# Four rows of an expert's matrix per partition: 2 MB transfers into nine double slots

## The chip, the cores and the metric

The kernel runs on one core of one Trainium2 chip. A core has five engines that run side by side: TensorE (PE; its weight loads are listed apart as PEld), VectorE (DVE), ScalarE (ACT), GpSimd (POOL) and SyncE (SP), which issues most of the DMA transfers; 16 DMA engines move the data. The metric is the device time of one execution in microseconds, as the median of several runs.

## What is computed

One decoder layer for 256 tokens of width 1024 in f32: sliding-window attention and a gated chunk mixer, a mixture of experts, a second mixer with a recurrent state, and a feed-forward block. The change lies in the mixture of experts. 32 experts have three 1024 x 1024 matrices each (384 MB of f32 in all), and each token goes to four experts:

```python
def routed_experts(x, w_router, b_router, w_gate, b_gate, w_up, b_up, w_down, b_down):
    logits = (xt @ w_router + b_router).astype(jnp.float32)
    top_vals, top_idx = lax.top_k(logits, TOP_K)          # TOP_K = 4
    gates = jax.nn.softmax(top_vals, axis=-1)
    ...
    def expert_block(args):
        xb, e = args
        gt = jnp.minimum(xb @ w_gate[e] + b_gate[e], SWIGLU_LIMIT)
        up = jnp.clip(xb @ w_up[e] + b_up[e], -SWIGLU_LIMIT, SWIGLU_LIMIT)
        hid = gt * jax.nn.sigmoid(SWIGLU_ALPHA * gt) * (up + 1.0)
        return hid @ w_down[e] + b_down[e]
    ...
    out = jnp.zeros((T + 1, D), x.dtype).at[row_tok].add(y_rows * row_gate[:, None])[:T]
```

## The kernel before

The stages follow each other: `front` (attention, gated mixer, router; up to about 125 us), `moe` (the experts; to about 1068 us), `mixer2` (to about 1365 us) and `ffn2` (to the end).

**Weights.** Every expert matrix is read as four *pieces* of 1 MB, 384 pieces in all. `expert_pieces` (L634) lists them in the order of use: gate and up of expert e, then down of expert e-1, and so on. A piece holds 256 rows of the matrix, and its view `(i p x) c -> i p x c` with x = 2 puts rows 256i + 2p and 256i + 2p + 1 into partition p, so that each partition reads one run of 8 KB. The pieces go into 18 slots of 128 x 2048 f32 in a ring (`SLOTS_A`, six, and `SLOTS_B`, twelve). The first 18 pieces are issued while `front` still runs, by `pump` (L1259); all later ones by `fetch`, which calls `piece` (L182; the DMA is L188, on SyncE's queue). `ahead(n)` (L923) calls `fetch` for all pieces up to 18 beyond those already used, once per expert ahead of gate and up (8 pieces) and once ahead of down (4 pieces). So a transfer is issued as soon as the matmuls on the slot's former piece are done. The DMAs of a queue share eight semaphores in turn, so that one is issued only when the eighth before it has landed (the DMAHW waits in the rows of order below).

**Products.** Tokens are chosen per expert by a one-hot matrix. For each pair of experts, `gather` (L710) multiplies h with it, with h as the weights that TensorE loads: 8 chunks of 128 columns by 2 halves of the tokens, 32 matmuls (tiles `tr<-oh,h` and `sc<-oh,h`). Since partition p holds every second row of a piece, chunk k takes every second column of h, by `pairs(k)` (L628). In the same manner `hidden_t` (L768) transposes the hidden values sg of one expert by 4 instructions (L81, `tr<-ident,sg`). `product` then runs 32 matmuls on the four pieces of a matrix (tiles g, u and y, L77), 8 on each.

**The overflow branch.** After expert 15 (`REST`), all engines meet at a loop over tokens that didn't fit (L851), which runs no times here. Before it SyncE waits for every transfer issued so far (206 pieces, of which 192 are used by then). The loop cuts the experts' stage into two segments: pieces 18 to 205 ahead of it, 206 to 383 behind it. Behind the loop the gather of the next pair comes first.

**After the experts.** The constants of the next stage go into two ring slots (`small`), and the front and the later stages use the same slots for their own weights (`raw_slots`, `half_slots`, given out by `pump`).

Of the kernel before, what the change touches and what calls it, by code (L numbers as in the profile page):

```python
# [12 lines left out]
F32 = mybir.dt.float32  # L13
F32R = mybir.dt.float32r
# [16 lines left out]

SLOTS_A = "r8 c1 c0 c2 c3 c4".split()
SLOTS_B = "r0 r1 r2 r3 r4 r5 r6 r7 h0 h1 h2 h3".split()

REST = 15
RING_A = len(SLOTS_A)
FFN_RAW, FFN_HALF = 4, 4
# [18 lines left out]
def bcast_rows(ap, n, parts=128):  # L56
    return bass.AP(tensor=ap.tensor, offset=ap.offset, ap=[[0, parts], [1, n]])


class Net:  # L60
# [120 lines left out]

    def piece(self, src, name="w"):  # L182

        pool, i = self.rings[self.turn % len(self.rings)]
        self.turn += 1
        t = pool.tile([128, 2048], F32, tag=i, name=self.nm(name))
        for view, ap in src(t):
            self.nc.sync.dma_start(view, ap)  # L188
        return t

    def front(self, fctx):
# [18 lines left out]

        slot = {i: (p, f"s{i}") for p, names in ((self.pa, SLOTS_A), (self.pb, SLOTS_B)) for i in names}
        cs = [slot[f"c{i}"][0].tile([128, 2048], F32, tag=f"sc{i}", name=f"front_c{i}") for i in range(5)]

# [39 lines left out]
        nf = len(spec)  # L253
        work = self.expert_pieces()
        spec += [(2, src) for _, src in work[:len(slot)]]
        L = {}
# [74 lines left out]
        def freed():  # L331
            self.freed()
            if len(self.half) == len(halves):
                self.raw_slots += self.half_slots
                self.half_slots = []
                self.pump()

# [267 lines left out]
        assert len(self.raw) == len(spec) and not self.raw_slots  # L605
        self.rings = [self.held[nf + i] for i in range(len(slot))]
        self.turn = len(slot)
        self.work = work
        self.got = {key: t for (key, _), t in zip(work, self.raw[nf:])}

# [16 lines left out]
    @staticmethod  # L627
    def pairs(k):  # L628


        i, x = divmod(k, 2)
        return slice(256 * i + x, 256 * i + 256, 2)

    def expert_pieces(self):  # L634

        r = []
        for e in range(NE + 1):
            for x, names in ((e, ("w_gate", "w_up")), (e - 1, ("w_down",)), (e, ("w_down",))):
                if x in range(NE) and (len(names) == 2 or (x == e) == (x == REST)):
                    for nme in names:  # L640
                        v = self.a[nme][0, x].rearrange("(i p x) c -> i p x c", p=128, x=2)
                        r += [((x, nme, i), v[i]) for i in range(4)]
        return r

    def fetch(self, n):

        for key, src in self.work[len(self.got):n]:
            t = self.piece(lambda t: [(t.rearrange("p (k c) -> p k c", k=2), src)])
            self.got[key] = t.rearrange("p (k c) -> p k c", k=2)

    def moe(self, mctx):
# [52 lines left out]
        def gather(b):  # L704
            xg[b] = m2.tile([128, KC, EB * CAP], F32, tag="xg", bufs=1, name=self.nm("xg"))
            for c0 in range(0, KC, 4):
                p = bank(*(("sc", 2) if c0 else ("tr", 1)), [128, 4, EB * CAP])
                for c in range(4):
                    for t in range(NT):
                        self.mm(p[:, c, :], self.h[:, t, self.pairs(c0 + c)],  # L710
                                oh[b][:, t].rearrange("p e s -> p (e s)"), start=t == 0, stop=t == NT - 1)
                nc.vector.tensor_copy(xg[b][:, c0:c0 + 2, :], p[:, 0:2])
                nc.scalar.copy(xg[b][:, c0 + 2:c0 + 4, :], p[:, 2:4])
# [50 lines left out]
        def hidden_t(sg):  # L764
            hidT = m2.tile([128, 4, 2, CAP], F32, tag="hidT", bufs=1, name=self.nm("hidT"))
            p = bank("tr", 1, [128, 4, 128])
            for j in range(4):
                self.tr(p[:, j, :], sg[:, self.pairs(j)])  # L768
            nc.scalar.copy(hidT[:, 0:2].rearrange("p j f s -> p j (f s)"), p[:, 0:2])  # L769
            nc.vector.tensor_copy(hidT[:, 2:4].rearrange("p j f s -> p j (f s)"), p[:, 2:4])  # L770
            return hidT
# [7 lines left out]
        def weights_of(e, nme):  # L779
            return lambda k: self.got[e, nme, k // 2][:, k % 2, :]  # L780

# [67 lines left out]
        def overflow():  # L849
            n = nc.values_load(lists["num"][0:1, 0:1], min_val=0, max_val=NL - 1)  # L850
            with tc.For_i(0, n, 1) as i:  # L851
# [15 lines left out]
                for k in range(KC):  # L867
                    for t in range(NT):
                        self.mm(p[:, k, :], self.h[:, t, self.pairs(k)], oh[:, t], start=t == 0, stop=t == NT - 1)
                nc.vector.tensor_copy(xo, p)  # L870

                def weights(nme):
                    def f(k):
                        w = m2.tile([128, D], F32, tag="wx", bufs=1, name=self.nm("wx"))
                        rows = a[nme][0, bass.ds(e, 1)].rearrange("o (i p x) c -> i x (o p) c", p=128, x=2)
                        nc.sync.dma_start(w, rows[k // 2, k % 2])
# [98 lines left out]

        def small(*names):
            while self.rings[self.turn % len(self.rings)][0] is self.pa:
                self.turn += 1
            t = self.piece(lambda t: [(t[:, i * D:(i + 1) * D], bcast_rows(a[nme], D)) for i, nme in enumerate(names)])
            return t[:, 0:D], t[:, D:2 * D]  # L980
# [220 lines left out]
    def stream(self):  # L1201
# [23 lines left out]
        for f in range(NF + 2):  # L1225
            for q in range(3):
# [3 lines left out]
                if u % 2 == 0:  # L1230
# [5 lines left out]
                               else (lambda t, x=x: t[:, x:x + 1, :])))  # L1236
        self.pieces(spec, halves, [(self.pa, f"s{i}") for i in SLOTS_A[:2]])
        self.half_slots = [(self.pa, f"s{i}") for i in SLOTS_A[2:]]
        self.low = [self.nc.gpsimd]
# [8 lines left out]
    def pump(self):  # L1248

        nc = self.nc  # L1250
        while True:
            while self.raw_slots and len(self.raw) < len(self.spec):
                r = len(self.raw)
                k, src = self.spec[r]
                pool, tag = self.held[r] = self.raw_slots.pop(0)
                n = src.shape[2]
                t = pool.tile([128, 2048], F32, tag=tag, name=self.nm("w"))[:, :k * n]
                t = t.rearrange("p (k c) -> p k c", k=k)
# [8 lines left out]
            k, n = src.shape[1:]  # L1267
            pool, tag = slot = self.half_slots.pop(0)
            t = pool.tile([128, 2, 1024], F32R, tag=tag, name=self.nm("wp"))[:, :, :k * n]
            t = t.rearrange("p q (k c) -> p q k c", k=k)  # L1270
# [650 lines left out]
    def ffn2(self):  # L1921
# [3 lines left out]
        with ExitStack() as c:  # L1925
# [79 lines left out]
```

## Time and profile before

| | us |
|---|---|
| median of 3 runs | 1569.32 (1568.11 to 1570.33) |
| the profiled execution | 1571.36 |
| its span | 1569.3 |
| TensorE's matmuls busy | 1423.9 (91%) |
| VectorE busy | 600.2 (38%) |
| ScalarE busy | 364.1 (23%) |

The page cuts the span into 40 slices of 39 us. For each it gives what the DMA engines moved in GB/s. The rows further below come from this and from closer views of the trace: stretches with their DMA share, waits, and the timeline of an engine, where equal instructions in a row stand in one line with their count. A time in brackets behind a row is the idle time before it, with what ended it.

### The profile page before, as it was taken

What the parts mean: (1) busy time and instruction counts of PE and PEld (TensorE: products, weight loads), DVE (VectorE), ACT (ScalarE), POOL (GpSimd) and SP (SyncE); (2) the same over time, 40 slices, a digit from 0 to 9 for tenths busy, and PEclk for the clock granted to TensorE, in tenths of its full rate; (3) what the DMA queues carried; (4) which work ended last, traced back from release to release, by engine and by line L of the source; (5) the groups of instructions that cost most, each with busy time, mean ns of one, the idle gap of its engine ahead of it and who ended that gap; (6) DMA issues with size and microseconds to landing.
All of it is one profiled execution on the core that took longest, in us unless ns stands there. A gap on an engine that the chain in (4) does not pass through costs nothing. (4 is left out here: it accounts for less than half of the span.)

```text
span 1569.3 us, 19400 instructions
## 1 busy us (share of the span) xinstructions
PE 1423.9 (91%) x7904; PEld 825.2 (53%) x7904; DVE 600.2 (38%) x1087; ACT 364.1 (23%) x607; POOL 177.6 (11%) x155
## 2 busy tenths in 40 slices
PE   8779999999998865999999989997987999999998
PEld 7664333333333222333333332326876887799998
DVE  4882121122121110121223221215578556876664
ACT  4551010100101000001001010003544233365552
POOL 4630000000000002000000000003443214200000
PEclk9988999999999997999999999998999999999999
DMA  9786999999999998999999999993523124675540
GB/s 303 277 330 259 422 418 422 421 421 421 421 421 422 421 421 311 422 421 421 421 421 421 421 421 421 421 420 119 177 88 117 32 76 172 209 247 178 193 143 27
DMA packets 119279, 491.14 MB, mean 313 GB/s; under 512 B 16391, under 2 KB 46791, under 8 KB 70036
## 3 DMA queue, kind: packets, MB, share of 16 engines
q1 hardware_dynamic: 118304, 489.02, 78.6%
q8 instruction: 63, 1.03, 0.3%
q0 software_dynamic: 512, 0.20, 0.1%
q10 hardware_dynamic: 372, 0.66, 0.1%
q14 instruction: 28, 0.23, 0.0%
HBM read 488.34 MB, written 1.51 MB: 312 GB/s over the span
## 5 line engine op out<-in xcount | busy, mean ns | idle before, releaser
L77 PE MATMUL g<-w,xg 128*64 128x512 f32 x1024 | 239.1, 618 | 4.8 <-DMA w<-in_w_gate_dram 4.8
L77 PE MATMUL u<-w,xg 128*64 128x512 f32 x1024 | 228.6, 594 | 9.9 <-DMA w<-in_w_up_dram 9.9
L77 PE MATMUL y<-w,hidT 128*64 128x512 f32 x1024 | 226.5, 594 | 1.9 <-ACT hidT L769 1.0
L1272 DVE TENSOR_TENSOR wp<-w,wp 128x1024 fp32r<-128x1024 f32 x115 | 153.0, 1355 | 106.7 <-ACT wp L1271 106.6
L1271 ACT CAST wp<-w 128x1024 fp32r<-128x1024 f32 (+1 forms) x148 | 151.6, 1038 | 167.1 <-PE pj L77 63.7
L77 PEld LDWEIGHTS u<-w,xg 128*64 128x64 f32 x1024 | 70.2, 137 | 157.8 <-issue 125.3
L77 PEld LDWEIGHTS g<-w,xg 128*64 128x64 f32 x1024 | 73.8, 143 | 149.5 <-issue 129.1
L77 PEld LDWEIGHTS y<-w,hidT 128*64 128x64 f32 x1024 | 70.9, 137 | 151.1 <-issue 139.9
L1272 POOL TENSOR_TENSOR wp<-w,wp 128x1024 fp32r<-128x1024 f32 (+1 forms) x33 | 78.6, 2386 | 575.0 <-DMA w<-in_w_in_dram 447.7
L777 ACT COPY y<-y 64x512 f32<-64x512 f32 x64 | 37.1, 580 | 369.1 <-PE y L77 368.7
L757 DVE TENSOR_SCALAR g<-g 128x512 f32<-128x512 f32 x32 | 22.1, 691 | 228.1 <-PE g L77 228.1
L770 DVE COPY hidT<-tr 128x256 f32<-128x256 f32 x32 | 13.6, 424 | 230.4 <-ACT hidT L769 230.4
L760 DVE TENSOR_SCALAR g<-u 128x512 f32<-128x512 f32 x32 | 22.1, 691 | 168.2 <-PE u L77 168.1
L77 PE MATMUL pj<-wp,h2p 128*128 128x512 f32 x336 | 82.9, 402 | 2.1 <-DVE wp L1272 1.9
L758 ACT ACTIVATE sg<-g 128x512 f32<-128x512 f32 x32 | 20.2, 630 | 253.3 <-DVE g L757 253.3
L77 PEld LDWEIGHTS pj<-wp,h2p 128*128 128x128 f32 x336 | 62.8, 191 | 18.5 <-DVE wp L1272 2.7
L77 PE MATMUL a<-h3p,wp 128*128 128x256 f32 x528 | 66.9, 283 | 0.5 <-DVE h3p L1307 0.5
L77 PEld LDWEIGHTS a<-h3p,wp 128*128 128x128 f32 x528 | 66.0, 191 | 2.2 <-DVE h3p L1307 0.7
L77 PE MATMUL b<-h3p,wp 128*128 128x256 f32 x528 | 66.9, 283 | 0.0
L77 PEld LDWEIGHTS b<-h3p,wp 128*128 128x128 f32 x528 | 64.9, 192 | 0.0
L77 PE MATMUL tr<-oh,h 128*128 128x128 f32 x256 | 37.7, 306 | 29.9 <-DVE oh L700 29.9
L77 PE MATMUL sc<-y,ogT 128*128 128x512 f32 x124 | 62.5, 619 | 2.5 <-ACT y L777 1.4
(527 smaller groups left out, 1609.0 us busy)
## 6 DMA issues: line engine op xcount, KB each, us to landing
w<-in_w_gate_dram SPq DMA_DIRECT2D x128, 1024.0 KB, 19.8
w<-in_w_up_dram SPq DMA_DIRECT2D x128, 1024.0 KB, 19.8
w<-in_w_down_dram SPq DMA_DIRECT2D x128, 1024.0 KB, 19.8
w<-in_w_in_dram SPq DMA_DIRECT2D x27, 1024.0 KB, 5.1
w<-in_w_ffn_up_dram SPq DMA_DIRECT2D x22, 1024.0 KB, 5.2
w<-in_w_ffn_down_dram SPq DMA_DIRECT2D x11, 1024.0 KB, 7.7
w<-in_w_out_dram SPq DMA_DIRECT2D x8, 1024.0 KB, 8.2
w<-in_w_branch_b_dram SPq DMA_DIRECT2D x2, 1024.0 KB, 4.9
```

The source lines that it names most:

```text
L77: return self.nc.tensor.matmul(out, lhsT, rhs, start=start, stop=stop)
L757: nc.vector.tensor_scalar(g1, pg, 7.0, None, op0=OP.min)
L758: nc.scalar.activation(sg, g1, AF.Sigmoid, scale=1.702)
L760: nc.vector.tensor_scalar(g1, pu, -7.0, 7.0, op0=OP.max, op1=OP.min)
L770: nc.vector.tensor_copy(hidT[:, 2:4].rearrange("p j f s -> p j (f s)"), p[:, 2:4])
L777: nc.scalar.copy(yv[64 * i:64 * i + 64, hf * 512:(hf + 1) * 512], py[64 * hf:64 * hf + 64, :])
L1271: nc.scalar.copy(t[:, 0], src)
L1272: self.low[j % len(self.low)].tensor_tensor(t[:, 1], src, t[:, 0].bitcast(F32), op=OP.subtract)
```

## The change

Each partition gets four neighbouring rows of a matrix: the view has x = 4, a half of a matrix (2 MB) is one transfer, and each partition reads one run of 16 KB. The ring has nine slots of 128 x 4096 in place of eighteen of 128 x 2048. The first 18 pieces and the last four are still transfers of 1 MB: a piece is then half of a partition's four rows (a run of 8 KB out of each 16 KB), and it goes into half of a double. `ahead` counts in doubles, so each call issues the same bytes as before. Since partition p holds rows 4p to 4p + 3 of a half, chunk k now takes every fourth column of h and of sg (`rows_of`), in as many instructions as before. The constants of the next stage go into one double.

```diff
-SLOTS_A = "r8 c1 c0 c2 c3 c4".split()
-SLOTS_B = "r0 r1 r2 r3 r4 r5 r6 r7 h0 h1 h2 h3".split()
+PAIRS = "r2r3 r4r5 r6r7 r8c1 c0c2 c3c4 r0r1 h2h3 h0h1".split()
+PAIRS_A = PAIRS[3:6]
+
+EARLY = 2 * len(PAIRS)
...
-    def piece(self, src, name="w"):
-
-        pool, i = self.rings[self.turn % len(self.rings)]
-        self.turn += 1
-        t = pool.tile([128, 2048], F32, tag=i, name=self.nm(name))
-        for view, ap in src(t):
-            self.nc.sync.dma_start(view, ap)
-        return t
+    def double(self, name, dtype=F32):
+
+        return (self.pa if name in PAIRS_A else self.pb).tile([128, 4096], dtype, tag=name, name=self.nm("w"))
+
+    @staticmethod
+    def halved(t):
+        return [Slot(t[:, 2048 * x:2048 * x + 2048]) for x in range(2)]
...
-    def pairs(k):
-
-
-        i, x = divmod(k, 2)
-        return slice(256 * i + x, 256 * i + 256, 2)
-
-    def expert_pieces(self):
+    def rows_of(k):
+
+
+        i, x = divmod(k, 4)
+        return slice(512 * i + x, 512 * i + 512, 4)
+
+    def expert_quarters(self):
...
-                        v = self.a[nme][0, x].rearrange("(i p x) c -> i p x c", p=128, x=2)
-                        r += [((x, nme, i), v[i]) for i in range(4)]
+                        v = self.a[nme][0, x].rearrange("(i p x) c -> i p x c", p=128, x=4)
+                        r += [((x, nme, q), v[q // 2][:, 2 * (q % 2):2 * (q % 2) + 2, :]) for q in range(4)]
...
     def fetch(self, n):
 
-        for key, src in self.work[len(self.got):n]:
-            t = self.piece(lambda t: [(t.rearrange("p (k c) -> p k c", k=2), src)])
-            self.got[key] = t.rearrange("p (k c) -> p k c", k=2)
+        while self.turn < n and 2 * self.turn < len(self.work):
+            u = 2 * self.turn
+            t = self.double(PAIRS[self.turn % len(PAIRS)]).rearrange("p (k c) -> p k c", k=4)
+            self.turn += 1
+            (key, src), (key1, src1) = self.work[u:u + 2]
+            if u < len(self.work) - 4:
+                e, nme, q = key
+                v = self.a[nme][0, e].rearrange("(i p x) c -> i p x c", p=128, x=4)
+                self.nc.sync.dma_start(t, v[q // 2])
+            else:
+                self.nc.sync.dma_start(t[:, 0:2], src)
+                self.nc.sync.dma_start(t[:, 2:4], src1)
+            self.have(key, t[:, 0:2])
+            self.have(key1, t[:, 2:4])
...
-                        self.mm(p[:, c, :], self.h[:, t, self.pairs(c0 + c)],
+                        self.mm(p[:, c, :], self.h[:, t, self.rows_of(c0 + c)],
...
-                self.tr(p[:, j, :], sg[:, self.pairs(j)])
+                self.tr(p[:, j, :], sg[:, self.rows_of(j)])
...
-            self.fetch(done[0] + len(self.rings))
-            done[0] += n
+            self.fetch(done[0] + len(PAIRS))
+            done[0] += 2 * n
...
-            ahead(4)
+            ahead(1)
...
-            ahead(8)
+            ahead(2)
...
-        self.ln2g, self.ln2b = small("ln2_g", "ln2_b")
-        self.n1g, self.junk = small("norm1_g_2")
+        while PAIRS[self.turn % len(PAIRS)] in PAIRS_A:
+            self.turn += 1
+        t = self.double(PAIRS[self.turn % len(PAIRS)])
+        self.ln2g, self.ln2b, self.n1g, self.junk = (t[:, i * D:(i + 1) * D] for i in range(4))
+        for view, nme in ((self.ln2g, "ln2_g"), (self.ln2b, "ln2_b"), (self.n1g, "norm1_g_2")):
+            nc.sync.dma_start(view, bcast_rows(a[nme], D))
```

On SyncE, where the first pieces of the ring's second round are issued (w_down is expert 0's, then come gate and up of expert 1; a wait for DMAHW is for an earlier transfer on that semaphore, a wait for PE is for the slot), the rows before are:

```order
L1259 DMA w_1066<-in_w_down_dram 128x2048 [waits DMAHW2_49,PE_49]
L1259 DMA w_1074<-in_w_down_dram 128x2048 [waits DMAHW3_49,PE_49]
L188 DMA w_1295<-in_w_down_dram 128x2048 [waits DMAHW4_49,PE_49]
L188 DMA w_1297<-in_w_down_dram 128x2048 [waits DMAHW5_49,PE_49]
L188 DMA w_1299<-in_w_gate_dram 128x2048 [waits DMAHW6_49,PE_49]
L188 DMA w_1301<-in_w_gate_dram 128x2048 [waits DMAHW7_49,PE_49]
```

In the changed kernel the same stretch reads:

```order
L1290 DMA w_1028<-in_w_down_dram 128x2048 [waits DMAHW2_49,PE_49]
L1290 DMA w_1028<-in_w_down_dram 128x2048 [waits DMAHW3_49]
L676 DMA w_1250<-in_w_down_dram 128x4096 [waits DMAHW4_49,PE_49]
L676 DMA w_1252<-in_w_gate_dram 128x4096 [waits DMAHW5_49,PE_49]
L676 DMA w_1254<-in_w_gate_dram 128x4096 [waits DMAHW6_49,PE_49]
```

One row of 128x4096 stands for two of 128x2048, and its wait for PE covers both halves of the slot.

On SyncE just ahead of the overflow branch (`onum` is the number of tokens that didn't fit), the rows before are:

```order
L188 DMA w_3099<-in_w_gate_dram 128x2048 [waits DMAHW4_49,PE_49]
L188 DMA w_3101<-in_w_gate_dram 128x2048 [waits DMAHW5_49,PE_49]
L188 DMA w_3103<-in_w_up_dram 128x2048 [waits DMAHW6_49,PE_49]
L188 DMA w_3105<-in_w_up_dram 128x2048 [waits DMAHW7_49,PE_49]
L850 TENSOR_LOAD onum [waits DVE_49]
L850 ISA x2
```

And in the changed kernel:

```order
L676 DMA w_2828<-in_w_gate_dram 128x4096 [waits DMAHW7_49,PE_49]
L676 DMA w_2870<-in_w_gate_dram 128x4096 [waits DMAHW0_49,PE_49]
L676 DMA w_2872<-in_w_up_dram 128x4096 [waits DMAHW1_49,PE_49]
L882 TENSOR_LOAD onum [waits DVE_49]
L882 ISA x2
```

The same two pieces of w_up are the last ones ahead of the branch, now as one transfer. On the other engines the instructions stand in the same order as before.

## Rows read from the trace of the kernel before

**Rows 1.** The page's 40 slices: GB/s that the DMA engines moved.

```profile
GB/s 303 277 330 259 422 418 422 421 421 421 421 421 422 421 421 311 422 421 421 421 421 421 421 421 421 421 420 119 177 88 117 32 76 172 209 247 178 193 143 27
```

**Rows 2.** Stretches: engines' busy us (instructions), granted clock, DMA share, GB/s.

```profile
200.00:300.00 100.00, 95.76 (x454) 37.15 (x456) 22.24 (x50) 9.71 (x20) 2.26 (x4) 0.98 1.01 420
1098.00:1100.00 2.00, 2.00 (x20) 2.00 (x19) 1.16 (x3) 0.88 (x3) 1.97 (x1) 1.00 1.03 399
1146.00:1148.00 2.00, 2.00 (x10) 1.65 (x9) 2.00 (x3) 0.78 (x1) 0.59 (x1) 1.00 1.02 386
```

**Rows 3.** SyncE's queue: line, waited for: us in total, times, longest us.

```profile
SPq L188 <- DMA w<-in_w_down_dram: 204.7, 100, 2.5
...
SPq L188 <- PE g L77: 97.1, 42, 19.6
```

**Rows 4.** SyncE's timeline at the experts' start, and one stretch there.

```profile
127.14 2.04 SPq L188 DMA_DIRECT2D w<-in_w_down_dram  x2
...
150.66 2.24 SPq L188 DMA_DIRECT2D w<-in_w_up_dram  x2
...
150.00:155.00 5.00, 5.00 (x24) 1.52 (x22) 0.00 (x0) 0.00 (x0) 0.00 (x0) 0.91 0.65 215
```

**Rows 5.** Timeline around the overflow branch, TensorE.

```profile
573.76 3.89 PE L77 MATMUL sc<-y,ogT 128*128 128x512 f32 x8 [0.68 <-ACT y L777]
606.66 3.78 PE L77 MATMUL tr<-oh,h 128*128 128x128 f32 x16 [29.01 <-DVE oh L700]
```

**Rows 6.** TensorE's timeline in segment 2: gathers and the end of u 31.

```profile
753.54 2.15 PE L77 MATMUL tr<-oh,h 128*128 128x128 f32 x16
...
757.41 4.12 PE L77 MATMUL sc<-y,ogT 128*128 128x512 f32 x8
...
809.30 2.15 PE L77 MATMUL tr<-oh,h 128*128 128x128 f32 x16
...
863.36 2.15 PE L77 MATMUL tr<-oh,h 128*128 128x128 f32 x16
...
922.16 2.15 PE L77 MATMUL tr<-oh,h 128*128 128x128 f32 x16
...
981.82 2.15 PE L77 MATMUL tr<-oh,h 128*128 128x128 f32 x16
...
1039.60 1.94 PE L77 MATMUL u<-w,xg 128*64 128x512 f32 x8 [0.56 <-DMA w<-in_w_up_dram]
1041.47 1.98 PE L77 MATMUL sc<-y,ogT 128*128 128x512 f32 x4
```

**Rows 7.** TensorE's waits from 127 to 606 us.

```profile
PE u L77 <- DMA w<-in_w_up_dram: 4.0, 8, 0.6
PE g L77 <- DMA w<-in_w_gate_dram: 2.8, 6, 0.6
...
PE y L77 <- DMA w<-in_w_down_dram: 0.4, 1, 0.4
```

**Rows 8.** Weight loads of transposes (L81): ns min/median/max, first and last start.

```profile
L81 PEld LDWEIGHTS tr<-ident,sg x128: 194/209/226, 145.5 to 1052.9; 128*128 128x128 f32 x128
...
L81 PEld LDWEIGHTS tr<-ident,og x32: 138/142/144, 139.3 to 999.5; 128*128 128x128 f32 x32
```

**Rows 9.** TensorE's timeline in mixer2: contiguous transposes.

```profile
1178.65 0.60 PE L81 MATMUL s<-ident,cs 128*128 128x128 f32 x4
1179.08 0.60 PE L81 MATMUL s<-ident,e 128*128 128x128 f32 x4
```

**Rows 10.** VectorE's groups by form, 1160 to 1190 us: busy us, mean ns.

```profile
L1543 DVE TENSOR_TENSOR z<-s,mask 128x384 f32<-128x384 f32 x8 | 3.9, 544 | 0.3 <-PE s L77 0.3
...
L1565 DVE TENSOR_TENSOR h<-h,rsi 128x512 f32<-128x512 f32 x1 | 0.7, 673 | 0.0
L1550 DVE TENSOR_TENSOR TA<-TA 128x225 f32<-128x225 f32 x1 | 0.6, 565 | 0.0
...
L1550 DVE TENSOR_TENSOR TA<-TA 128x144 f32<-128x144 f32 x1 | 0.4, 405 | 0.0
```

More of the change, by code (lines that the diff above doesn't have):

```diff
@@ L29 @@
 NEG = -1e30
-SLOTS_A = "r8 c1 c0 c2 c3 c4".split()
-SLOTS_B = "r0 r1 r2 r3 r4 r5 r6 r7 h0 h1 h2 h3".split()
+PAIRS = "r2r3 r4r5 r6r7 r8c1 c0c2 c3c4 r0r1 h2h3 h0h1".split()
+PAIRS_A = PAIRS[3:6]
+EARLY = 2 * len(PAIRS)
 REST = 15
-RING_A = len(SLOTS_A)
 FFN_RAW, FFN_HALF = 4, 4
@@ L57, in bcast_rows, with __init__, room @@
     return bass.AP(tensor=ap.tensor, offset=ap.offset, ap=[[0, parts], [1, n]])
+class Slot:
+    def __init__(self, view=None, pool=None, tag=None, dtype=F32):
+        self.view, self.pool, self.tag, self.dtype = view, pool, tag, dtype
+    def room(self, name):
+        return self.view if self.pool is None else self.pool.tile([128, 2048], self.dtype, tag=self.tag, name=name)
 class Net:
@@ L208, in front @@
         self.warm(bank("o", [128, 128]), warm, WARM[2])
-        slot = {i: (p, f"s{i}") for p, names in ((self.pa, SLOTS_A), (self.pb, SLOTS_B)) for i in names}
-        cs = [slot[f"c{i}"][0].tile([128, 2048], F32, tag=f"sc{i}", name=f"front_c{i}") for i in range(5)]
+        slot = {}
+        for name in PAIRS:
+            slot[name[:2]], slot[name[2:]] = self.halved(self.double(name, F32R if name[0] == "h" else F32))
+        cs = [slot[f"c{i}"].view for i in range(5)]
         def carve(i, at, shape):
@@ L253, in front @@
         nf = len(spec)
-        work = self.expert_pieces()
-        spec += [(2, src) for _, src in work[:len(slot)]]
+        work = self.expert_quarters()
+        spec += [(2, src) for _, src in work[:EARLY]]
         L = {}
@@ L332, in freed @@
             self.freed()
[L333 to L336, printed above, removed]
+            for name in PAIRS[-2:]:
+                pair = [slot[name[:2]], slot[name[2:]]]
+                if len(self.half) == len(halves) and all(i in self.half_slots for i in pair):
+                    self.half_slots = [i for i in self.half_slots if i not in pair]
+                    slot[name[:2]], slot[name[2:]] = self.halved(self.double(name))
+                    through(name[:2], name[2:])
         def through(*names):
@@ L605, in front @@
         assert len(self.raw) == len(spec) and not self.raw_slots
[L606 to L609, printed above, removed]
+        order = [slot[h] for t in PAIRS for h in (t[:2], t[2:])]
+        assert [self.held[nf + i] for i in range(EARLY)] == order
+        self.work, self.turn, self.got = work, len(PAIRS), {}
+        for (key, _), t in zip(work, self.raw[nf:]):
+            self.have(key, t)
     def split_biases(self, bf):
@@ L640, in expert_pieces, with have @@
                     for nme in names:
-                        v = self.a[nme][0, x].rearrange("(i p x) c -> i p x c", p=128, x=2)
-                        r += [((x, nme, i), v[i]) for i in range(4)]
-        return r
+                        v = self.a[nme][0, x].rearrange("(i p x) c -> i p x c", p=128, x=4)
+                        r += [((x, nme, q), v[q // 2][:, 2 * (q % 2):2 * (q % 2) + 2, :]) for q in range(4)]
+        return r
+    def have(self, key, t):
+        for x in range(2):
+            self.got[key[:2] + (2 * key[2] + x,)] = t[:, x, :]
     def fetch(self, n):
-        for key, src in self.work[len(self.got):n]:
-            t = self.piece(lambda t: [(t.rearrange("p (k c) -> p k c", k=2), src)])
-            self.got[key] = t.rearrange("p (k c) -> p k c", k=2)
+        while self.turn < n and 2 * self.turn < len(self.work):
[12 more added lines that the diff above has]
+            self.have(key1, t[:, 2:4])
     def moe(self, mctx):
@@ L779, in weights_of @@
         def weights_of(e, nme):
-            return lambda k: self.got[e, nme, k // 2][:, k % 2, :]
+            return lambda k: self.got[e, nme, k]
         def gate_up(e):
@@ L868, in overflow @@
                     for t in range(NT):
-                        self.mm(p[:, k, :], self.h[:, t, self.pairs(k)], oh[:, t], start=t == 0, stop=t == NT - 1)
+                        self.mm(p[:, k, :], self.h[:, t, self.rows_of(k)], oh[:, t], start=t == 0, stop=t == NT - 1)
                 nc.vector.tensor_copy(xo, p)
@@ L874, in f @@
                         w = m2.tile([128, D], F32, tag="wx", bufs=1, name=self.nm("wx"))
-                        rows = a[nme][0, bass.ds(e, 1)].rearrange("o (i p x) c -> i x (o p) c", p=128, x=2)
-                        nc.sync.dma_start(w, rows[k // 2, k % 2])
+                        rows = a[nme][0, bass.ds(e, 1)].rearrange("o (i p x) c -> i x (o p) c", p=128, x=4)
+                        nc.sync.dma_start(w, rows[k // 4, k % 4])
                         return w
@@ L974, in moe @@
         finish(NE - 1)
[L976 to L980, printed above, removed]
-        self.ln2g, self.ln2b = small("ln2_g", "ln2_b")
-        self.n1g, self.junk = small("norm1_g_2")
+        while PAIRS[self.turn % len(PAIRS)] in PAIRS_A:
[4 more added lines that the diff above has]
+            nc.sync.dma_start(view, bcast_rows(a[nme], D))
         flush(sums)
@@ L1236, in stream @@
                                else (lambda t, x=x: t[:, x:x + 1, :])))
-        self.pieces(spec, halves, [(self.pa, f"s{i}") for i in SLOTS_A[:2]])
-        self.half_slots = [(self.pa, f"s{i}") for i in SLOTS_A[2:]]
+        raw, *parts = PAIRS_A
+        self.pieces(spec, halves, self.halved(self.double(raw)))
+        self.half_slots = [h for t in parts for h in self.halved(self.double(t, F32R))]
         self.low = [self.nc.gpsimd]
@@ L1254, in pump @@
                 k, src = self.spec[r]
-                pool, tag = self.held[r] = self.raw_slots.pop(0)
+                slot = self.held[r] = self.raw_slots.pop(0)
                 n = src.shape[2]
-                t = pool.tile([128, 2048], F32, tag=tag, name=self.nm("w"))[:, :k * n]
+                t = slot.room(self.nm("w"))[:, :k * n]
                 t = t.rearrange("p (k c) -> p k c", k=k)
@@ L1267, in pump @@
             k, n = src.shape[1:]
-            pool, tag = slot = self.half_slots.pop(0)
-            t = pool.tile([128, 2, 1024], F32R, tag=tag, name=self.nm("wp"))[:, :, :k * n]
+            slot = self.half_slots.pop(0)
+            t = slot.room(self.nm("wp")).rearrange("p (q n) -> p q n", q=2)[:, :, :k * n]
             t = t.rearrange("p q (k c) -> p q k c", k=k)
@@ L1932, in bank @@
                 return ps.tile(shape, F32, tag=tag, bufs=bufs, name=self.nm(tag))
-            self.raw_slots += [(ph, f"r{i}") for i in range(FFN_RAW)]
+            self.raw_slots += [Slot(pool=ph, tag=f"r{i}") for i in range(FFN_RAW)]
             self.pump()
@@ L1942, in ffn2 @@
             self.low = [V]
-            self.half_slots += [(ph, f"h{i}") for i in range(FFN_HALF)]
+            self.half_slots += [Slot(pool=ph, tag=f"h{i}", dtype=F32R) for i in range(FFN_HALF)]
             self.pump()
```

## The prediction

> **What bounds the kernel now.** I read the slices of the page first, then the speed by stretch, then who waits for whom. From 125 to 1041 us the experts' 384 MB pass through the core, and the slices of GB/s stand at 420 to 422 in all that time but for the one at 155 and the one at 600 [rows 1]; 200 to 300 us give 420 GB/s at a share of 1.01, so all 16 DMA engines are full [rows 2]. SyncE's queue waits there for an earlier transfer to land (204.7 us in 100 waits for w_down's alone), more seldom for TensorE to give a slot back (97.1 us at g) [rows 3]. One piece of 1 MB takes 1048576 / 420,000 = 2.49 us.
>
> TensorE is busy nearly as long, and it depends on the segment which of the two ends last. *Segment 1* (pieces 18 to 205, 188 pieces) ends at the overflow branch, which waits for every transfer: TensorE is through at 573.76 + 3.89 = 577.65 and its next matmul starts at 606.66, after 29.01 us of idling, while the last pieces land [rows 5]. With the 7.2 us that it loses to late pieces before (4.0 on u, 2.8 on g, 0.4 on y) [rows 7] its slack is near 36 us. *Segment 2* (170 pieces up to the last of w_up 31) begins with 14 pieces already in the slots, and TensorE eats this lead. The gathers at L77 mark the pairs of experts: 753.54, 809.30, 863.36, 922.16, 981.82, and 1041.47 at the end of u 31. Two unhindered pairs last 55.76 and 54.06 us, 54.9 in the mean; the last three last 58.80, 59.66 and 59.65, and the last u pieces have waits of 0.56 us [rows 6]. 24 pieces by 2.49 us are 59.8: there the DMA is the bound, and before it TensorE is. So TensorE's slack in segment 2 is only 178.1 - 3 x 54.9 = 13.4 us (10.8 and 15.9 with either pair alone).
>
> **The change part by part.**
>
> *Longer runs.* 358 pieces (188 + 170) lie on the stream that the DMA bounds, 358 x 2.49 = 891 us. Runs of 2 KB go at 399 and 386 GB/s, of which I take 395; runs of 8 KB at 420 [rows 2]. Per KB and engine that is 41.5 and 39.0 ns, so each run has about 2.5 / (1/2 - 1/8) = 6.6 ns of its own, and runs of 16 KB would go at 39.0 - 6.6 / 16 = 38.6 ns or 424 GB/s, 1.05% less time: -9.4 us, -4.9 in segment 1 and -4.5 in segment 2. No row shows runs of 16 KB of this kind; the ends are 0 (a run is cut at 8 KB anyway) and -13.1 us (1.5%, by the slower row, 386). I take -9.4, from the mean of the rows. The Trainium skill weighs this otherwise: "DMA: Bandwidth & Descriptors", section "Why small descriptors are slow (HBM only)", has a fixed cost of about 3 cycles a packet beside 32-byte beats. Worked out from that page, an estimate, 256 beats become 512 beside 3 cycles, a gain of 0.6% or 5 us in place of 9.4; the rows differ from it, for it would put 2 KB runs 3.4% below 8 KB ones and they are 6% below.
>
> *Doubles at the start.* A slot now comes free when two pieces are consumed. Two pieces of w_down are issued from 127.14 on, the second at 127.14 + 2.04 - 0.33 = 128.85; later the queue stands for TensorE until 150.66, the next issue is at 150.66 + 2.24 - 0.33 = 152.57, and the DMA share is 0.65 in between [rows 4]. A double goes out with the second piece of each couple, so the stream starts 1.7 us later, and restarts 1.9 us later. In the order of SyncE's instructions there stands one row of 128x4096 for two of 128x2048, each behind one wait for PE. At the overflow branch nothing is added: of 206 pieces issued 192 are consumed by then, so four slots are free, and two doubles go out at once.
>
> *Doubles at the end.* u 31 waits for its last pieces [rows 6]; as 2 MB they land together, so the first of them is there one piece of 2.49 us later than it was, and two pieces of TensorE's work (1041.47 - 1039.60 = 1.87 us each) remain in place of one: +1.9 us, where the DMA is still the bound then. Both terms lie within 0 and 2.5 us.
>
> *Fewer SyncE instructions, slots in the front stage, constants in one double.* 604 rows become 423; SyncE is not on the path. The early pieces are issued as before, in halves of doubles, ahead of the experts; the constants' loads lie beside the last products with w_down, which TensorE has still to do after u 31. Nothing, and with that cover gone about one piece, 2.5 us.
>
> *The stride of TensorE's weight loads.* To match four rows per partition, `gather` and `hidden_t` take every fourth column of h and sg in place of every second: 32 instructions a pair and 4 an expert, 40 a pair. That is the part that decides. The stride already costs something: the load of sg, at stride 2, lasts 194 to 226 ns (median 209), that of og, contiguous and otherwise the same, 138 to 144 [rows 8]: 67 ns more. Most of it is hidden behind the matmul: 32 instructions of the gather take 757.41 - 753.54 = 3.87 us, 121 ns each [rows 6], and contiguous transposes (1179.08 - 1178.65) / 4 = 108 ns [rows 9]. So at stride 2 the load has just come out from behind its matmul, and whatever stride 4 adds is seen in full. No row shows TensorE at stride 4. From below: 0, if a load costs the same at any stride. From above: 0.134 us, if the 67 ns double each time the span doubles. The nearest row at a wide stride is VectorE's: L1550 with sources 64 B apart takes (565 - 405) / (225 - 144) = 1.98 ns an element, contiguous products of two operands (673 - 544) / 128 = 1.01 [rows 10]. That factor of 1.96 on 108 ns gives 212 (+0.091 over 121), on 121 gives 237 (+0.116). I take **+0.10 us**, the middle.
>
> The Trainium skill has a rule that speaks against the change: "SBUF — State Buffer", section "Door 1: The DMA port swizzle (why `[64,N]` ≈ `[32,N]`)", says that SBUF is read in lines of 16 bytes, with full bandwidth only from two hits on a line. Stride 2 of f32 has two hits and would be free by it, stride 4 has one and would not; the trace agrees only in part, since stride 2 costs 67 ns here.
>
> **The sum.** Segment 1: 320 x 0.10 = 32.0 us. TensorE alone would be through at 577.65 + 32.0 - 7.2 = 602.5, still ahead of the pieces. The stream starts later by 1.9 and by the first gather (32 x 0.10 = 3.2, ahead of the first g) and gains 4.9: +0.2. Segment 2: 8 gathers and 60 transposes, 316 x 0.10 = 31.6, minus 13.4 of slack: +18.2. TensorE then ends after the pieces, so neither the longer runs nor the last double counts there. Expert 31's transposes add 0.4. In all +18.8. The profiled execution took 1571.36 us (its span is 1569.3), which gives 1590.2; it lies 2.0 above the median of the runs, 1569.32, so on the median **1588**. The two prices by VectorE's factor with the two ends of the slack, 0.091 with 15.9 and 0.116 with 10.8, give 1582 and 1595; the upper end of the price, 0.134, gives +31.5 in segment 2 and 7 more in segment 1, where 43 us exceed the slack: 1608.
>
> **The rivals.**
> 1. *Loads at stride 4 cost what they cost at stride 2.* For it: in the gather the load's surplus is small already (121 against 108 ns). Then the stream decides in both segments: -9.4 + 1.9 + 1.9 = -5.6 us, 1563.7, and with the other end of the runs' gain 1560. This is the case that is faster. It decides below a price of 0.047 us an instruction: there 316 + 32 of them cost 16.4 us, which is the slack of 13.4 and the 3.0 gained in segment 1.
> 2. *Half the price*, 0.05 us: segment 1 gains 4.9 - 1.9 - 1.6 = 1.4 us, segment 2 loses 15.8 - 13.4 = 2.4: +1.0, 1570. No row stands for just this price; it is the middle of ends.
> 3. *The longer run moves no faster* (a run is cut on the way, or the bound lies elsewhere), and the loads cost nothing: +1.9 + 1.9 = +3.8, 1573. Against it: the step from 2 KB to 8 KB shows in the rows.
>
> **How the numbers follow.** Forecast (its own range 1579 to 1601) 0.50: the rows of TensorE and of VectorE both show that distance between elements costs, and segment 2 has little slack. Rival 1 0.34, rival 2 0.10, rival 3 0.06. A measurement of this kernel can tell about 0.2%, 3.1 us, from no change. Faster: rival 1 and a little of rival 2, 0.35. Within 0.2%: most of rival 2 and a little of the others, 0.11. Slower: the forecast, rival 3 and the rest, 0.54. The range takes in rival 1 nearly whole and the forecast but for its far end: 1558 to 1600; the forecast's own stands above.
>
> **What would show it.** In the profile of the changed kernel: the weight loads of `tr<-oh,h` and `tr<-ident,sg` near 300 ns, 16 matmuls of a gather in 3.5 us or more in place of 2.15, pairs of 58 to 60 us right after the overflow branch, and no waits for w_up at the end. If 16 matmuls still take 2.15 us, rival 1 holds, and the rate by stretch then tells 1 from 3: 424 GB/s against 420. A wait for 2 MB pieces in the middle of a segment, with the DMA share below 1, would be something that none of this has: nine slots too coarse for the stream.

## The result: slower by 1%

The changed kernel takes 1583.69 us (1581.82 to 1592.99, 5 runs) where the kernel before takes 1569.15 in the same runs: a ratio of 1.0102 (1.0073 to 1.0130), or +14.5 us. The profiled execution is the slowest of the five, 1592.99 us with a span of 1591.3; TensorE's mean granted clock was 0.965 in it and 0.969 to 0.974 in the others, and the five times fall as the clock rises. The profiled execution before had 0.964. The segments are read below from these two profiles, which differ by 22.0 us in all.

The changed kernel's page, the 40 slices of GB/s as in [rows 1], now of 39.8 us:

```profile
GB/s 298 284 314 248 383 422 411 417 431 428 427 427 428 428 428 300 426 412 423 403 407 428 427 428 428 427 355 60 159 113 116 30 77 133 214 252 182 194 151 27
```

The slices around 150 to 320 us stand at 383, 422, 411 and 417 where they were 422, 418, 422 and 421; later most stand at 427 or 428, which is more than the 421 before. So the stream did become faster, and it is interrupted more often. Three stretches (columns as in [rows 2]: DMA share and GB/s at the end) show both sides:

```profile
150.00:155.00 5.00, 5.00 (x20) 1.42 (x18) 0.00 (x0) 0.00 (x0) 0.00 (x0) 0.74 0.07 30
175.00:180.00 5.00, 5.00 (x26) 1.86 (x22) 0.00 (x0) 0.49 (x1) 0.00 (x0) 1.00 0.72 239
400.00:500.00 100.00, 96.03 (x430) 41.63 (x431) 17.92 (x31) 9.41 (x20) 0.00 (x0) 1.00 1.01 428
```

From 150 to 155 us the DMA engines now stand nearly still (0.07, where [rows 4] has 0.65), and 175 to 180 is a second gap. SyncE's queue shows what it waits for (us in total, times, longest):

```profile
SPq L676 <- PE y L89: 330.4, 56, 14.8
SPq L676 <- PE g L89: 309.2, 62, 22.4
SPq L676 <- PE u L89: 188.3, 60, 3.3
```

828 us of waiting, all for TensorE. Before, [rows 3] had waits for landing transfers at the top. This total alone does not show that the stream starves: with the nine double slots and no stride (the second experiment) the queue still waits 681 us for TensorE, while the stream is full. The gaps above are the evidence. What makes TensorE late is seen in the weight loads (busy us and mean ns, with the shapes apart; the first row is the kernel before):

```profile
L77 PEld LDWEIGHTS tr<-oh,h 128*128 128x128 f32 x256 | 34.4, 213 | 42.2 <-DVE oh L700 29.8 <-issue 11.6 <-ACT sg L758 0.8
...
L89 PEld LDWEIGHTS tr<-oh,h 128*128 128x128 f32 x256 | 60.9, 328 | 27.9 <-DVE oh L732 15.5 <-issue 11.6 <-ACT sg L790 0.8
...
L93 PEld LDWEIGHTS tr<-ident,sg 128*128 128x128 f32 x128 | 18.1, 210 | 28.3 <-issue 28.3
```

A load of `tr<-oh,h` lasts 328 ns where it lasted 213; those of `tr<-ident,sg` stay at 210, as in [rows 8]. On TensorE's timeline (start, us, count; the first row is the kernel before, the others are the changed one and answer to [rows 5] and [rows 6]):

```profile
125.21 7.03 PE L77 MATMUL g<-w,xg 128*64 128x512 f32 x32
...
125.43 7.03 PE L89 MATMUL g<-w,xg 128*64 128x512 f32 x32
...
611.16 4.10 PE L89 MATMUL tr<-oh,h 128*128 128x128 f32 x16 [14.68 <-DVE oh L732]
...
771.76 4.00 PE L89 MATMUL tr<-oh,h 128*128 128x128 f32 x16
775.59 3.90 PE L89 MATMUL sc<-oh,h 128*128 128x128 f32 x16
779.33 4.11 PE L89 MATMUL sc<-y,ogT 128*128 128x512 f32 x8
...
1056.95 7.03 PE L89 MATMUL u<-w,xg 128*64 128x512 f32 x32
1063.91 1.98 PE L89 MATMUL sc<-y,ogT 128*128 128x512 f32 x4
```

A gather from its first row to the next group takes 779.33 - 771.76 = 7.57 us where it took 3.87. At the overflow branch TensorE idles 14.68 us in place of 29.01, and the last u runs in one piece without a wait for w_up: behind the branch TensorE is the bound to the end.

By segments, from the starts of these rows and those of [rows 5] and [rows 6]: first g to the first gather behind the branch 485.7 us (611.16 - 125.43; before 606.66 - 125.21 = 481.4), from there to the end of u 31 452.8 us (before 434.8), and the rest of the span 527.4 (before 527.8). So of the profile's 22 us 18 are lost in segment 2 and 4 in segment 1.

### The profile page after: what moved, and what is told of

Its sections match the earlier page's. It is cut to its first block, busy times and chain, and to the rows that moved or that the text cites. A ratio compares the mean times of both kernels' runs of the same rounds, so it can differ in the third digit from the quotient of the medians.

```text
span 1591.3 us, 19047 instructions
## 1 busy us (share of the span) xinstructions
PE 1477.3 (93%) x7904; PEld 883.9 (56%) x7904; DVE 598.8 (38%) x1087; ACT 363.8 (23%) x607; POOL 178.4 (11%) x155
## 2 busy tenths in 40 slices
DMA packets 93213, 491.11 MB, mean 309 GB/s; under 512 B 13495, under 2 KB 43895, under 8 KB 67140
## 5 line engine op out<-in xcount | busy, mean ns | idle before, releaser
L1302 ACT CAST w<-w 128x1024 fp32r<-128x1024 f32 (+1 forms) x116 | 118.6, 1035 | 149.3 <-PE pj L89 63.4
L1303 DVE TENSOR_TENSOR w<-w,w 128x1024 fp32r<-128x1024 f32 x83 | 114.1, 1391 | 84.3 <-ACT w L1302 84.1
L1303 POOL TENSOR_TENSOR w<-w,w 128x1024 fp32r<-128x1024 f32 (+1 forms) x33 | 79.4, 2411 | 589.0 <-ACT w L1302 583.1
L89 PE MATMUL pj<-w,h2p 128*128 128x512 f32 x336 | 83.0, 402 | 1.8 <-DVE w L1303 1.8
L89 PE MATMUL tr<-oh,h 128*128 128x128 f32 x256 | 64.2, 409 | 15.6 <-DVE oh L732 15.6
L89 PEld LDWEIGHTS tr<-oh,h 128*128 128x128 f32 x256 | 60.9, 328 | 27.9 <-DVE oh L732 15.5
L89 PEld LDWEIGHTS pj<-w,h2p 128*128 128x128 f32 x336 | 62.6, 190 | 18.5 <-DVE w L1303 2.6
L89 PE MATMUL sc<-oh,h 128*128 128x128 f32 x256 | 62.2, 398 | 0.0
L89 PEld LDWEIGHTS sc<-oh,h 128*128 128x128 f32 x256 | 61.3, 329 | 0.0
L760 DVE TENSOR_TENSOR x<-x,sc 128x512 f32<-128x512 f32 x60 | 41.0, 686 | 28.4 <-PE sc L89 28.4
```

What stands on the lines that cost most here:

```text
L89: return self.nc.tensor.matmul(out, lhsT, rhs, start=start, stop=stop)
L760: nc.vector.tensor_tensor(dst, dst, pp[dh], op=OP.add)
L1302: nc.scalar.copy(t[:, 0], src)
L1303: self.low[j % len(self.low)].tensor_tensor(t[:, 1], src, t[:, 0].bitcast(F32), op=OP.subtract)
```

## The experiments

The theory is that the gather's weight loads at a stride of four columns cost TensorE about 3.7 us a pair of experts, and that this is a loss only where it exceeds what TensorE has to spare. The main rival is that nine coarse slots and 2 MB transfers starve the stream. The three parts of the change (16 KB runs, 2 MB slots, stride 4) can be had apart.

### The stride alone

```diff
-        i, x = divmod(k, 2)
-        return slice(256 * i + x, 256 * i + 256, 2)
+        i, x = divmod(k, 4)
+        return slice(512 * i + x, 512 * i + 512, 4)
...
-                        v = self.a[nme][0, x].rearrange("(i p x) c -> i p x c", p=128, x=2)
-                        r += [((x, nme, i), v[i]) for i in range(4)]
+                        v = self.a[nme][0, x].rearrange("(i p x) c -> i p x c", p=128, x=4)
+                        r += [((x, nme, q), v[q // 2][:, 2 * (q % 2):2 * (q % 2) + 2, :]) for q in range(4)]
```

> The kernel before with four rows per partition, but still 1 MB transfers with runs of 8 KB into 18 slots: the stride of 4 in gather and hidden_t comes alone. Theory (the gather's weight loads decide, 241 ns an instruction for 121): 16 matmuls of a gather in about 4.0 us as in the changed kernel, the transposes of sg unchanged at 209 ns, no waits for w_up at the end of segment 2, and +14 to +20 us over the kernel before, 1583 to 1589. Rival (nine coarse slots and 2 MB transfers cost the time): 1568 to 1573, as nothing of that is in it.

Measured: 1586.14 us, a ratio of 1.0104 (1.0088 to 1.0121), as slow as the whole change within the intervals. The stream is at the old rate and TensorE is as late as in the changed kernel (stretch, columns as above; weight loads; timeline):

```profile
300.00:400.00 100.00, 96.09 (x443) 39.66 (x442) 17.69 (x30) 10.15 (x20) 0.00 (x0) 1.00 1.01 421
```

```profile
L77 PEld LDWEIGHTS tr<-oh,h 128*128 128x128 f32 x256 | 60.9, 328 | 31.4 <-DVE oh L700 19.0 <-issue 11.6 <-ACT sg L758 0.8
...
L81 PEld LDWEIGHTS tr<-ident,sg 128*128 128x128 f32 x128 | 18.1, 210 | 28.3 <-issue 28.3
```

```profile
612.98 4.10 PE L77 MATMUL tr<-oh,h 128*128 128x128 f32 x16 [18.18 <-DVE oh L700]
...
1062.47 1.98 PE L77 MATMUL sc<-y,ogT 128*128 128x512 f32 x4
```

Segment 2 takes 1062.47 - 612.98 = 449.5 us, +14.7, and segment 1 485.8 (from its first g at 127.15), +4.4. The other 4.2 us of this profile's 23.3 lie ahead of the first g (1.9) and behind u 31 (2.3). There are 18 slots of 1 MB here and no 2 MB transfer: the rival falls as the main cause, and the stride alone makes a loss in both segments. In segment 2 the changed kernel lost 3.2 us more; the part on the prediction says where most of it lies.

### The changed kernel without the stride

h is put in the order of the chunks once, in place, behind the sum that reads it last in its first order. Every gather but the first then loads contiguous columns; the transposes of sg keep the stride of 4.

```diff
                 start_sum()
+                for t in range(NT):
+                    hs = m2.tile([128, D], F32, tag="wx", bufs=1, name=self.nm("hs"))
+                    nc.scalar.copy(hs.rearrange("p (i x c) -> p i x c", i=2, x=4),
+                                   self.h[:, t].rearrange("p (i c x) -> p i x c", i=2, x=4))
+                    nc.scalar.copy(self.h[:, t], hs)
...
-                        self.mm(p[:, c, :], self.h[:, t, self.rows_of(c0 + c)],
+                        cols = slice(128 * (c0 + c), 128 * (c0 + c) + 128) if b else self.rows_of(c0 + c)
+                        self.mm(p[:, c, :], self.h[:, t, cols],
```

> The changed kernel, with h put in the order of the chunks once (four copies on ScalarE behind the sum that starts acc, while expert 1 runs), so that every gather but the first loads contiguous columns; 2 MB transfers and nine slots stay. Theory: 16 matmuls of a gather in 2.0 us or less, the stream bounds again, at 427 GB/s for 420, 1.6% of 891 us = -14, and +3.8 for the doubles at start and end: about 1559 (1554 to 1563), faster than both kernels. Rival (coarse slots): 1575 or more, still slower than before.

Measured: 1559.95 us (1554.48 to 1562.57, 4 runs), a ratio of 0.9926 (0.9898 to 0.9954): faster than both kernels. The stream is at 427 and bounds again (stretches; timeline with the waits in brackets):

```profile
175.00:180.00 5.00, 3.13 (x18) 1.35 (x16) 0.76 (x2) 1.90 (x4) 0.00 (x0) 1.00 0.99 423
300.00:400.00 100.00, 95.75 (x464) 37.02 (x462) 20.60 (x35) 10.39 (x22) 0.00 (x0) 1.00 1.01 427
```

```profile
603.11 3.78 PE L89 MATMUL tr<-oh,h 128*128 128x128 f32 x16 [27.09 <-DVE oh L732]
...
640.94 2.05 PE L89 MATMUL tr<-oh,h 128*128 128x128 f32 x16
642.83 1.95 PE L89 MATMUL sc<-oh,h 128*128 128x128 f32 x16
...
1028.26 3.65 PE L89 MATMUL u<-w,xg 128*64 128x512 f32 x16 [1.26 <-DMA w<-in_w_up_dram]
1031.84 1.98 PE L89 MATMUL sc<-y,ogT 128*128 128x512 f32 x4
```

16 rows of a gather take 2.05 us, TensorE idles 27.09 us at the branch, and u 31 waits 1.26 us for its last 2 MB. Segment 1 takes 603.11 - 125.54 = 477.6 us (-3.9) and segment 2 428.7 (-6.1). So the DMA side of the change, without the stride, is a gain of some 10 us, and the stride turned it into a loss. Of the changed kernel's two gaps, the one at 175 to 180 us is gone (share 0.99 for 0.72), so that one is the second gather's. The one at 150 to 155 us remains (0.09, for 0.07), so the later gathers do not make it. The share there is 0.35 with the stride alone and 0.42 with the doubles alone (next experiment), for 0.65 before: each of the two makes part of it.

### The doubles without longer runs

```diff
-                v = self.a[nme][0, e].rearrange("(i p x) c -> i p x c", p=128, x=4)
-                self.nc.sync.dma_start(t, v[q // 2])
+                v = self.a[nme][0, e].rearrange("(j i p x) c -> j p i x c", i=2, p=128, x=2)
+                self.nc.sync.dma_start(t.rearrange("p (i x) c -> p i x c", i=2), v[q // 2])
```

The pieces' view and `rows_of` go back to two rows (x = 2, step 2) with it.

> The changed kernel with two rows per partition: one transfer of 2 MB carries two blocks with runs of 8 KB, nine slots, stride 2 in gather and hidden_t as before. Theory: 420 GB/s as before, loads of 196 ns as before, and only the doubles' cost at start and end, +2 to +5 us: 1571 to 1574. If the transfer's size gives the speed and not the run, 427 GB/s and about 1560. Rival (coarse slots): about 1583.

Measured: a ratio of 1.0005 (0.9991 to 1.0020), no difference that can be told (medians 1572.23 and 1569.64). The stretch, and the end of u 31:

```profile
300.00:400.00 100.00, 96.02 (x458) 37.35 (x456) 19.91 (x34) 10.25 (x21) 0.00 (x0) 0.98 1.01 421
```

```profile
607.53 3.78 PE L89 MATMUL tr<-oh,h 128*128 128x128 f32 x16 [28.16 <-DVE oh L732]
...
1039.17 3.65 PE L89 MATMUL u<-w,xg 128*64 128x512 f32 x16 [1.31 <-DMA w<-in_w_up_dram]
1042.75 1.99 PE L89 MATMUL sc<-y,ogT 128*128 128x512 f32 x4
```

With 2 MB transfers of 8 KB runs the rate stays at 421, so it is the run that gives 427 and not the transfer's size. The pages of the two profiles bear out that the longer run is moved whole: they count 116381 DMA packets here and 93213 in the changed kernel, 23168 fewer, which is half of the 46336 runs of 8 KB that the 181 whole doubles hold. Segment 1 takes 607.53 - 125.41 = 482.1 us (+0.7), segment 2 435.2 (+0.4): the coarse slots cost about 1 us in the experts' segments, and no cost can be told in the time.

### Strides from 1 to 8

In the kernel before, each of the eight chunks of a gather reads h at another stride, 1 to 8 columns, on a line of its own (L713 to L728), and the four transposes of sg at 1 to 4 (L785 to L788).

```diff
+                        M(p[:, 0, :], self.h[:, t, 0:128], o[t], **f[t])
...
+                        M(p[:, 3, :], self.h[:, t, 0:1024:8], o[t], **f[t])
...
+            X(p[:, 0, :], sg[:, 0:128], self.ident)
...
+            X(p[:, 3, :], sg[:, 0:512:4], self.ident)
```

> The kernel before with strides of 1 to 8 columns in the eight chunks of a gather, each on a line of its own, and 1 to 4 in the four transposes of sg (the columns are the wrong ones, so its output is not the reference's). Theory (cost goes by 16-byte lines): two instructions take about 0.22 us at stride 1, 0.24 at 2, 0.36 at 3, 0.48 at 4 and no more at 5 to 8; rival (cost goes with the span read): 0.96 at stride 8. Transposes: 209 ns at stride 2 and 4 alike as both kernels show; at stride 1 140 if the stride makes the difference to og, 209 if not.

Measured (1580.94 us in its one run): TensorE's timeline of one gather, a line per stride, and the loads of sg:

```profile
648.31 0.64 PE L715 MATMUL tr<-oh,h 128*128 128x128 f32 x4
648.78 0.86 PE L717 MATMUL tr<-oh,h 128*128 128x128 f32 x4
649.48 1.09 PE L719 MATMUL tr<-oh,h 128*128 128x128 f32 x4
650.41 1.06 PE L722 MATMUL sc<-oh,h 128*128 128x128 f32 x4
651.30 1.06 PE L724 MATMUL sc<-oh,h 128*128 128x128 f32 x4
652.20 1.10 PE L726 MATMUL sc<-oh,h 128*128 128x128 f32 x4
653.13 1.11 PE L728 MATMUL sc<-oh,h 128*128 128x128 f32 x4
```

```profile
L788 PEld LDWEIGHTS tr<-ident,sg 128*128 128x128 f32 x32 | 6.6, 206 | 0.0
...
L786 PEld LDWEIGHTS tr<-ident,sg 128*128 128x128 f32 x32 | 6.3, 198 | 0.0
...
L785 PEld LDWEIGHTS tr<-ident,sg 128*128 128x128 f32 x32 | 4.5, 140 | 28.3 <-issue 28.3
```

An f32 matmul that the program writes once stands twice in the trace, so each line has four rows for its two matmuls, and a gather's 16 matmuls stand as 32; the 32 matmuls that the text ahead of the prediction gives a gather and a product are such rows. From start to start a row takes 0.47 / 4 = 0.118 us at stride 2, 0.70 / 4 = 0.175 at 3, 0.93 / 4 = 0.233 at 4, and no more at 5 to 7 (0.22 to 0.23); the row of stride 8 lasts as long as that of 7 (1.11 and 1.10 us). That is the theory's curve: 128 columns of 4 bytes lie in 64, 96 and 128 lines of 16 bytes, and 0.175 / 96 and 0.233 / 128 are both 1.82 ns a line. At stride 2 this makes 0.117, just over the 0.108 that a matmul takes anyway. The rival, cost by the span read, would have doubled it again from 4 to 8. The transposes behave otherwise: 140 ns at stride 1, 198 to 206 at 2 to 4. Why stride 4 costs them nothing more stays open.

### The sorted copy in the kernel before

The same edit with i = 4 and x = 2, on 1 MB transfers, 8 KB runs and 18 slots.

```diff
+                    nc.scalar.copy(hs.rearrange("p (i x c) -> p i x c", i=4, x=2),
+                                   self.h[:, t].rearrange("p (i c x) -> p i x c", i=4, x=2))
+                    nc.scalar.copy(self.h[:, t], hs)
```

> The kernel before (1 MB transfers, runs of 8 KB, 18 slots) with the sorted copy of h, so that its gathers load contiguous columns too. Theory (the gain of the sorted doubles is the stream's 427 GB/s for 420): the gather falls from 3.9 to 3.5 us a pair, hidden by the stream, 421 GB/s as before, and 1567 to 1570, the same as before. Rival (contiguous loads are themselves the gain): 1560.

Measured: 1569.03 us, a ratio of 0.9998 (0.9988 to 1.0007). The gathers do load faster, and the stream is as before (timeline; stretch):

```profile
639.83 2.05 PE L77 MATMUL tr<-oh,h 128*128 128x128 f32 x16
```

```profile
300.00:400.00 100.00, 95.75 (x458) 36.88 (x456) 19.68 (x34) 10.25 (x21) 0.00 (x0) 0.98 1.01 421
```

Contiguous loads by themselves gain nothing, as long as the stream bounds; what the second experiment gained is the longer run's.

### Half the price

```diff
-                        self.mm(p[:, c, :], self.h[:, t, self.rows_of(c0 + c)],
+                        cols = slice(128 * (c0 + c), 128 * (c0 + c) + 128) if t else self.rows_of(c0 + c)
+                        self.mm(p[:, c, :], self.h[:, t, cols],
```

> The changed kernel with every second load of a gather contiguous (the columns of the second 128 tokens are the wrong ones, so its output is not the reference's): a pair's gather takes 16 x 0.24 + 16 x 0.11 = 5.6 us, 1.7 more than before for 3.9 more. Theory (a loss only beyond TensorE's slack of 13 to 16 us in segment 2): 8 x 1.7 = 13.7 us are just covered there, the stream is faster in segment 1, and the time is 1562 to 1570, not slower than before. Rival (the loss is proportional to the price): half of the changed kernel's way from 1560 to 1584, 1571 to 1577.

Measured: 1565.57 us, a ratio of 0.9976 (0.9963 to 0.9989), faster than before though a gather takes 5.60 us for 3.87, nearly half as long again:

```profile
599.16 3.90 PE L89 MATMUL tr<-oh,h 128*128 128x128 f32 x16 [20.91 <-DVE oh L732]
...
638.24 3.02 PE L89 MATMUL tr<-oh,h 128*128 128x128 f32 x16
641.10 2.91 PE L89 MATMUL sc<-oh,h 128*128 128x128 f32 x16
...
1034.08 1.98 PE L89 MATMUL sc<-y,ogT 128*128 128x512 f32 x4
```

3.02 us for 16 rows where before took 2.15. Segment 2 takes 1034.08 - 599.16 = 434.9 us, the same as before to 0.1, with no wait for weights at its end. Its gathers are 12.6 us longer in all than before (seven by 1.73, the one behind the branch by 0.52), so this price has just used up the slack. Segment 1 is 4.7 us shorter (476.7 from its first g at 122.43). In the changed kernel the gathers of segment 2 are 14.6 us longer still (seven by 1.97, the one behind the branch by 0.83), and the segment by 452.8 - 434.9 = 17.9: the other half of the price is lost whole, and about 3 us come from elsewhere, most of it from TensorE's clock, as shown below. So the loss in segment 2 is not proportional to the price; it begins where the slack ends.

## Why the prediction came true, step by step

The forecast was 1588, slower, through TensorE's loads; measured were 1583.7. By its steps:

- **The bound and the slack.** That the two segments have different limits, and that TensorE has only some 13 us to spare in segment 2, is what the half price shows: 12.6 us more of gathers there changed the segment by 0.1. But the ends of this slack, 10.8 and 15.9, came of the clock and not of the pairs: the pair of 55.76 us has a g that ran at a granted clock of 0.80 and took 8.73 us, where the other products of these two pairs take 7.03 to 7.09; that is the 1.70 us between them (the kernel before, timeline and stretch):

```profile
771.73 8.73 PE L77 MATMUL g<-w,xg 128*64 128x512 f32 x32
```

```profile
771.73:780.40 8.67, 8.67 (x36) 2.73 (x34) 0.00 (x0) 0.24 (x1) 0.00 (x0) 0.80 1.01 420
```

- **The price of the stride.** +0.10 us on 40 instructions a pair, 4.0 us; measured are 7.57 - 3.87 = 3.7 on the gather's 32 (0.116 each, the upper of the two values that VectorE's factor gave) and none on the 8 transposes. The two errors cancel, which is luck. Nor is the price the same at every clock: the gathers ahead of either segment's first products run at a lower granted clock (0.60 at 117.80 to 125 us and 0.65 at 606.66 to 613.90 in the kernel before), where 16 of their rows took 3.75 and 3.78 us at stride 2 already, and stride 4 made these two gathers only 1.6 and 1.35 us longer. The 67 ns between sg and og were indeed stride's, but stride 4 adds nothing to them, so the upper end built on their doubling had no ground.
- **The rule of the Trainium skill.** The forecast cited "SBUF — State Buffer" in the Trainium skill, section "Door 1: The DMA port swizzle (why `[64,N]` ≈ `[32,N]`)", for full bandwidth from two hits on a line of 16 bytes. The gather's rows agree: stride 2 costs 0.118 us a row, stride 4 0.233, wider strides no more. The transposes of sg do not go by it: their loads take longer from stride 2 on (198 ns for 140) and no longer at 4 (206).
- **Longer runs.** 424 GB/s were forecast, 427 to 428 measured, 1.6% for 1.05%. On 358 pieces that is 14 us in place of 9.4, beyond the end of 13.1 that the slower row gave. The second experiment's segments got 10.0 of it; most of the rest is missing in segment 1, which begins with a longer gap (0.09 for 0.65 at 150 to 155 us). The 2 KB rows came from short stretches of another stage, and a line through two lengths of run is a poor guide to a third. The forecast's estimate by the Trainium skill, "DMA: Bandwidth & Descriptors", section "Why small descriptors are slow (HBM only)" (0.6%), is off by more.
- **The doubles.** +3.8 us were forecast at start and end; the doubles alone cost 0.7 and 0.4 us in the segments, and the time rose by 0.05%, which its interval does not tell from none. Why the longer gap at the start (0.42 for 0.65) costs so little in the end was not tried; u 31 waits 1.31 us for its last 2 MB where it had waited 0.56 for each 1 MB.
- **Segment 1.** Forecast +0.2, measured +4.3: the step that failed. Of the +0.2, 3.2 stood for the first gather, which comes ahead of the measured segment, so like for like the miss is -3.0 against +4.3. The sum let the stream lose only the first gather and the doubles' start. The stride alone costs 4.4 us there, and 8.2 on the faster stream (485.7 with it, 477.6 with the sorted copy). The second gather comes while the ring is still short of free slots, so its delay stops the stream once more (0.72 at 175 to 180 us, where the sorted copy has 0.99, and 411 and 417 GB/s in the slices after). TensorE was through with the segment at 611.16 - 14.68 = 596.5, ahead of the pieces as forecast (602.5), but its slack at the branch does not protect the stream at the segment's start: a slot that comes back late there costs at once.
- **Segment 2.** Forecast +18.2, measured +17.9 in the profiled execution; the mechanism was right, and that the number was met so closely is luck. The gathers became 27.2 us longer there in place of the 31.6 forecast for all 316 instructions; less the slack of 12.6 that makes 14.6, which is what the stride alone lost (14.7). Most of the other 3 us is the clock: six g of segment 2 took 8.17 to 8.73 us in place of 7.03 at granted clocks of 0.80 to 0.86, 9.0 us in all, against 6.3 with the stride alone, 6.6 in the kernel before and 6.7 at half the price. One of them in the changed kernel:

```profile
670.65 8.73 PE L89 MATMUL g<-w,xg 128*64 128x512 f32 x32
```

```profile
670.65:679.40 8.75, 8.75 (x36) 2.75 (x34) 0.00 (x0) 0.24 (x1) 0.00 (x0) 0.80 0.96 365
```

- **The sum.** +18.8 forecast, +22 in the profiled execution, +14.5 in the median. Against the profiled execution the forecast is short by 3.2, where segment 1 alone was missed by 4.1; against the median it is over by 4.3. The profiled run of the changed kernel had a lower clock than its other four (0.965 for 0.969 to 0.974); where TensorE bounds, its clock enters the time, and which part of the 9 us between its time and the median is the clock's was not tried. The range of 1558 to 1600 took in rival 1's 1560 too, so that it held says little; the forecast's own, 1579 to 1601, held as well. The upper price with the short slack sums to 1596, not 1595.

Rival 1 was wrong in its condition, not in its mechanism: where the stride is taken away the stream does decide, and the time falls to 1560, which it gave with the far end of the runs' gain (1563.7 with the middle). Rival 2's half price came out at 1565.6 for its 1570: segment 1 gained 4.7 us for its 1.4, and segment 2 lost 0.1 for its 2.4. Rival 3 falls: the longer run moves at 427 GB/s for 421.

## What to carry to other kernels

A layout that makes a transfer better also decides at which stride an engine reads what belongs to it: cost both, and cost the second per 16-byte line, 1.82 ns for each on TensorE's f32 weight loads here. An added cost on an engine that is not the bound was free in segment 2 until the slack of that stretch was used up, so find the slack by stretch (a half price, a sorted copy) before you weigh the gain. It is not free where a transfer waits for the slot that this engine gives back: segment 1 had some 36 us of slack and still lost. And where a strided read is repeated for 16 pairs, sorting the operand once (6.2 us on ScalarE, busy for 23% of the span before) kept the gain of the runs without the price of the stride: 1560 us.

## What the runs showed of the hardware

ScalarE's copies fit the line rule too. The copies that sort h (L983 and L985 of the second experiment, L951 of the fifth; 1024 columns, mean ns after the busy time):

```profile
L983 ACT COPY hs<-h 128x1024 f32<-128x1024 f32 x2 | 4.1, 2054 | 6.0 <-PE sc L89 6.0
...
L985 ACT COPY h<-hs 128x1024 f32<-128x1024 f32 x2 | 2.1, 1046 | 0.1
```

```profile
L951 ACT COPY hs<-h 128x1024 f32<-128x1024 f32 x2 | 2.3, 1130 | 5.0 <-PE sc L77 4.9
```

Read at stride 4 a copy takes 2054 ns, at stride 2 1130, contiguous 1046: with one element on each line of 16 bytes a copy takes nearly twice as long, with two 8% longer. And runs of 16 KB move at 427 to 428 GB/s where runs of 8 KB move at 421, in transfers of either 1 or 2 MB for the latter, with the DMA engines' share at 1.01 in each case.
